# Transposes of an output projection among the parts of its third sum, and a third block pair in the second gate/up product

## The chip, the cores and the metric

The kernel runs on one core of a Trainium2 chip. The core has TensorE (PE in the profile; its weight loads are PEld), VectorE (DVE), ScalarE (ACT), GpSimd (POOL) and SyncE (SP), each with a queue of its own that it works off in the order in which the scheduler put it at build time. The metric is the device time of one execution in microseconds, as a median over runs.

## What is computed

One layer of a decoder trunk for 256 tokens of width 2048, all in float32: half a SwiGLU feed-forward step, a mixing step with two kinds of heads, and a second half step.

```
x = x + 0.5 * swiglu(rmsnorm(x, ffn1_norm), ffn1_w_gate, ffn1_w_up, ffn1_w_down)   # 2048 -> 5632 -> 2048
h = rmsnorm(x, mix_norm)
a_q, a_k, a_v, m_q, m_k, m_v, m_o, m_i, m_f = split(h @ w_in)
y_a = diff_attention(a_q, a_k, a_v, ...)          # 4 heads, causal, normed per head
y_b = rmsnorm(mlstm(m_q, m_k, m_v, m_i, m_f)) * sigmoid(m_o)   # 4 heads
x = x + concat(y_a, y_b) @ w_out                  # the output projection
x = x + 0.5 * swiglu(rmsnorm(x, ffn2_norm), ffn2_w_gate, ffn2_w_up, ffn2_w_down)
out = rmsnorm(x, final_norm)
```

## The kernel before

**Products.** Every weight matrix is worked on in column blocks of 512 (CW). The rows are taken in k tiles of 128, two of them (UK) to a unit; 2048 rows are eight units. The activations stand transposed (k on the partitions), with the 256 tokens in two halves of 128 (hb). A float32 operand is split in a high part, rounded by ScalarE (L131: wh, xs, xt), and a low part, the remainder, by VectorE (L132: wl and the like). A product is three matmuls: high by high, low by high and high by low (`mms`, L180, L181 and L183). A unit done plainly for one column block costs 12 matmuls of 512 columns.

**Pairs in blocks.** `Paired` works two column blocks at once (wa and wb: gate and up, or two neighbouring blocks of a projection). For the first ns units it replaces the eight products of a 2 x 2 block (two k tiles, two token halves, two column blocks) with seven, at the price of sums of activations and of weights. The sums of activations are made by `sum_pair` and `sums` (four small passes of VectorE and another split); the four tiles and their four sums are A1, B1, A2, B2, S3, S1, S2, S4. The sums of weights are made in place in the tiles named raw. The block pair goes through these steps:

- `leading` goes through the block units by twos (`twos`). For each two it loads raw (L422 and L207), multiplies A1 (slot 0), makes the sums of raw on VectorE (L455), and for the two before it multiplies S1 and adds once more (`second_sum`: by a DMA that accumulates, L471, where there are over three block units, and by VectorE, L473, where there are fewer). Between these steps `Chain.run` lets the pair before, whose last part is still open (`stream`), go on unit by unit.
- `sums` multiplies S2 for each two, loads the rows of wa left out so far (the tile late, L487), adds them to raw by accumulating DMAs on POOL (L508), multiplies the late weights bare by A2 (`bare`), then copies and combines the accumulators (`copied`, L479; L512, L521) and multiplies S3.
- `second` does the remaining units of wa plainly and, between them, B2 and S4 of each block unit (`both`).
- `third` finishes wa, hands its two accumulators to `half`, and does the plain units of wb. It is the stream that the next pair's `run` takes along.

**Order.** The scheduler orders each engine's queue by the place of an instruction in the program, and by readiness in its own model of time. `tc.high_priority(offset=AHEAD)` moves instructions ahead by 400 places, `soon()` (used by `vec` and `act`) by 440. `tc.issue_after(newest[0].ins)` puts those TensorE instructions of its block behind the newest matmul that `mms` wrote. Transposes whose results a later step needs are kept as functions in lists: `pending`, taken by `flush(n)`, and `side`, one at a time by `aside(side)`.

**The second gate/up pair.** In the first feed-forward step the first gate block is plain, with the activations loaded and split on the way (`load_xt`, called two units at a time by `units`). The first up block is plain too; its last five units are the stream of the second pair. Five of the eight units of xp1 have activation sums (NP = 5). `sum_xt` makes them one after another: at load time for the units u >= KD // UK - NP_FIRST, queued on ScalarE behind the weight split three before; the others are put on `pending` and are all taken at u == FLUSH of the up stream. The second pair has NP_FIRST block units, later pairs have NP. The raw tiles come from a pool of five, and the first three pairs load them on SP's queue.

**The output projection.** `yT` has eight units: 0 to 3 from the attention heads (transposed by `y_transposes` from `side`), 4 to 7 from the other heads, put on `pending` by `gate_out`. `gate_out(0)` runs as the `half` and `gate_out(1)` as the end of the pair before, whose stream is worked off in the leading steps of the output projection's first pair. That pair is called with `gently=True` and has three block units (NP_OUT), so units 3 to 7 are plain. Each leading step ends with a `flush(1)` behind the newest matmul and with an `aside(side)`; `second` flushes one in each round.

Of the kernel before, what the change touches and what calls it, by code (L numbers as in the profile page):

```python
# [9 lines left out]
F32 = mybir.dt.float32  # L10
F32R = mybir.dt.float32r
BF16 = mybir.dt.bfloat16
AF = mybir.ActivationFunctionType
ALU = mybir.AluOpType
# [18 lines left out]
UK = 2  # L33
# [2 lines left out]
NPS_MIX = (3,4,4,4,3)  # L36
NP_QK = 2
NP_OUT = 3
NP_FIRST = 2
PARTS = (3, 2, 3, 3)  # L40
NP_DOWN = (3, 2, 3, 3)
LK = 4
AHEAD = 400
# [16 lines left out]
def tile_trunk_layer(ctx: ExitStack, tc: tile.TileContext, x, xt, par, bias_if, lamv, fnorm,  # L60
                     wg1, wu1, wd1, wqk0, wqk1, wqk2, win, wout, wg2, wu2, wd2, out):
    nc = tc.nc
# [14 lines left out]
    def nm(s):  # L77
        uid[0] += 1
        return f"{s}_{uid[0]}"
# [16 lines left out]
    def seeded(which):  # L96
        return ps_acc.tile([P, CW], F32, tag=f"acc{which}", name=nm(f"acc{which}"), bufs=1)
# [26 lines left out]
    def split_gain(src, gcol, hi, lo):  # L124

        nc.scalar.activation(hi, src, AF.Copy, scale=prm[:, gcol:gcol + 1])
        nc.vector.scalar_tensor_tensor(lo, src, prm[:, gcol:gcol + 1], hi.bitcast(F32),  # L127
                                       op0=ALU.mult, op1=ALU.subtract)

    def split(src, hi, lo):  # L130
        return (nc.scalar.copy(hi, src),  # L131
                nc.vector.tensor_tensor(out=lo, in0=src, in1=hi.bitcast(F32), op=ALU.subtract))  # L132
# [11 lines left out]
    def ahead_of_splits(i, ins, slack=SLACK):  # L144
        queued[i].append((len(splits) + slack, ins))
# [28 lines left out]
    newest = []  # L174
# [16 lines left out]
    def plain_pair(xp, j):  # L191

        t = slots.tile([P, 2, UK, S], F32R, tag="s", name=nm("xt"))
        xp[j] = tuple(t[:, i, :, :].rearrange("p a (b c) -> p (a b) c", b=NT) for i in range(2))
        return t[:, 0, :, :], t[:, 1, :, :]
# [3 lines left out]
    def flush(n=None):  # L199

        now = pending[:n]
        del pending[:n]
        for f in now:
            f()
# [77 lines left out]
    def chunk_to_xt(c, gbase, xp, ns, now=KD):  # L282


        def run(j):
            tr = ps_tr.tile([P, 2, S], F32, tag="tr", name=nm("tr"))
            for i in range(2):
                for hb in range(NT):
                    nc.tensor.transpose(tr[:, i, hb * P:(hb + 1) * P],
                                        xres[:, hb, (2 * j + i) * P:(2 * j + i + 1) * P], ident)  # L290
            with tc.high_priority(offset=AHEAD):
                if j < ns:
                    sum_pair(xp, j, gained(tr, prm[:, gbase + 2 * j:gbase + 2 * j + 2]), j >= now)
                else:
                    hi, lo = plain_pair(xp, j)
                    for i in range(2):
                        split_gain(tr[:, i, :], gbase + 2 * j + i, hi[:, i, :], lo[:, i, :])

        pending.extend(functools.partial(run, j) for j in (2 * c, 2 * c + 1))
# [4 lines left out]
    def gained(src, gain):  # L304
        g = wk("xg")
        for i in range(2):
            ahead_of_splits(0, act.activation(g[:, i * S:(i + 1) * S], src[:, i, :], AF.Copy, scale=gain[:, i:i + 1]))
        return g.rearrange("p (a b) -> p a b", b=P)

    def sum_tiles(xp, j):  # L310
        xp[j] = tuple(slots.tile([P, 8, P], F32R, tag="s", name=nm("xs")) for _ in range(2))
        return xp[j]

    def sum_pair(xp, j, g, put_off=False):
        hi, lo = sum_tiles(xp, j)
        split(g, hi[:, 0:4, :], lo[:, 0:4, :])
        (side.append if put_off else lambda f: f())(functools.partial(sums, g, hi, lo))

    def sums(g, hi, lo):
        s = wk("xsum").rearrange("p (a b) -> p a b", b=P)  # L320
        tt = nc.vector.tensor_tensor
        tt(out=s[:, 0:2, :], in0=g[:, 0:2, :], in1=g[:, 1:4:2, :], op=ALU.subtract)
        tt(out=s[:, 2, :], in0=s[:, 1, :], in1=g[:, 0, :], op=ALU.subtract)
        tt(out=s[:, 3, :], in0=g[:, 2, :], in1=s[:, 2, :], op=ALU.add)
        split(s, hi[:, 4:8, :], lo[:, 4:8, :])
# [36 lines left out]
    def wk(name):  # L362
        return work.tile([P, CW], F32, tag="w", name=nm(name))
# [11 lines left out]
    def soon(extra=40):  # L375
        return tc.high_priority(offset=AHEAD + extra)
# [14 lines left out]
    vec, act = Early(nc.vector), Early(nc.scalar)  # L391
    side, mid = [], []

    def aside(work):

        if work:
            work.pop(0)()

    class Paired:
# [94 lines left out]
                splits.append(split_weights(raw[:, 0:len(js), :], *t))  # L494
            mms([self.job(self.n11, j, A2, t, i, False, False, True) for i, j in enumerate(js)])

        def sums(self):

            ds = self.copied(self.d, wk("ds"))
            lates = []  # L500
            for js in self.twos:
                lates.append((js, self.late(js)))
                self.part(js, self.x, S2, 0)
                if self.rest[0] // UK not in self.xp:
                    flush(1)
                with tc.high_priority(offset=AHEAD):
                    for i, j in enumerate(js):
                        nc.gpsimd.dma_start(self.raws[j][:, 0, :], lates[-1][1][:, i, :], accum_op=ALU.add)  # L508
                if js[-1] == self.ns - 1:
                    us = self.copied(self.x, wk("us"))  # L510
                    with soon():
                        ahead_of_splits(1, nc.vector.tensor_tensor(out=self.d, in0=self.d, in1=us, op=ALU.subtract))  # L512
                if len(lates) > 1:
                    self.bare(*lates.pop(0))
            for js, raw in lates:
                self.bare(js, raw)
            for js in self.twos:
                self.part(js, self.x, S3, 1)
            self.n21 = self.copied(self.x, seeded(N21), SLACK - 2)
            with soon():  # L520
                ahead_of_splits(1, nc.vector.tensor_tensor(out=self.x, in0=ds, in1=self.x, op=ALU.subtract))  # L521
# [51 lines left out]
    class Chain:  # L573
# [7 lines left out]
        def run(self, p, half, end, last_units=1, gently=False):  # L581

            done = 0
            q = len(p.twos)
            first = p.leading()
            for i in range(q):
                while done < min(self.steps - 1, -(-(i + 1) * self.steps // (q + 1))):
                    next(self.stream)
                    done += 1
                next(first)  # L590
                if gently:
                    with tc.issue_after(newest[0].ins):
                        flush(1)
                else:
                    flush(1)
                aside(side)
            while done < self.steps - 1:
                next(self.stream)
                done += 1
            next(first, None)  # L600
            while done < self.steps:
                next(self.stream)
                done += 1
            self.end()
            p.sums()
            p.second(gently)
            self.put(p.third(half, last_units), len(p.rest) + 1, lambda: end(p.accs()))

# [6 lines left out]
    def ffn(chain, xp, rstd, wg, wu, wd, finish, first=None):  # L615
# [28 lines left out]
        for part, (n, ns) in enumerate(zip(PARTS, NP_DOWN)):  # L644
            hid = {}
            for c in range(n):
# [9 lines left out]
                else:  # L656
                    np_, queue = NP, nc.sync if done + c < ON_POOL else nc.gpsimd
                    if done + c == 1 and first is not None:
                        np_ = NP_FIRST
                        pending.extend([first[1]] * (NP - NP_FIRST))  # L660
                    chain.run(Paired(xp, wg[done + c], wu[done + c], KD, np_, queue=queue), half, end)
# [16 lines left out]
    def load_xt(u):  # L678
        k, i = u * UK, u % 2 * UK
        with tc.high_priority(offset=AHEAD):  # L680
# [14 lines left out]
            for t in range(UK):  # L695
                split_gain(raw[:, t, :], G_FFN1 + k + t, hi[:, t, :], lo[:, t, :])
        if u >= KD // UK - NP_FIRST:
            sum_xt()
# [6 lines left out]
    def sum_xt():  # L705

        raw, j, hi, lo = gs.pop(0)
        with tc.high_priority(offset=AHEAD), tc.issue_after(splits[-FIRST_SUMS][0].ins):
            sums(gained(raw, prm[:, G_FFN1 + j * UK:G_FFN1 + j * UK + UK]), hi, lo)
# [303 lines left out]
    for hb in range(NT):  # L1013
        for h in range(NH):
            i = hb * NH + h
# [49 lines left out]
    yT = {}  # L1065

    def y_transposes(halves, kt, gain):

        g = gain[:, kt % 8:kt % 8 + 2]
        tr = ps_tr.tile([P, 2, S], F32, tag="tr", name=nm("tr"))  # L1070
        for i in range(2):
            for hb in range(NT):
                nc.tensor.transpose(tr[:, i, hb * P:(hb + 1) * P], halves[hb][:, i * P:(i + 1) * P],
                                    ident)
        if kt // 2 < NP_OUT:
            sum_pair(yT, kt // 2, gained(tr, g))
            return
        hi, lo = plain_pair(yT, kt // 2)
        for i in range(2):
            act.activation(hi[:, i, :], tr[:, i, :], AF.Copy, scale=g[:, i:i + 1])  # L1080
            vec.scalar_tensor_tensor(lo[:, i, :], tr[:, i, :], g[:, i:i + 1], hi[:, i, :].bitcast(F32),
                                           op0=ALU.mult, op1=ALU.subtract)

    def weighted(h):
        ps = ps_acc.tile([P, NT, VD], F32, tag="acc", name=nm("av"))
# [43 lines left out]
    for c in (0, 2):  # L1129
        chain.run(Paired(yT, wout[c], wout[c + 1], KD, NP_OUT), functools.partial(finish_out, c),  # L1130
                  functools.partial(finish_out, c + 1),
                  gently=not c)
# [108 lines left out]
```

## Time and profile before

| what | value |
| --- | --- |
| median of three runs | 1772.36 us (1769.11 to 1775.43) |
| the profiled execution | 1771.66 us, of which its span is 1770.0 us |
| granted TensorE clock | 0.998 |
| POOL's busy share | 24% |
| read from HBM | 349.56 MB, 199 GB/s over the span |

The profile shows one execution. A busy share is that of an engine's whole span; a row of the timeline gives the start, the time shown for one or several instructions of a kind, the engine, the line, and in brackets the idle time ahead of it with the instruction that ended it. The time shown for a matmul is modelled and overlaps that of the next, and the same holds in part for VectorE and ScalarE, so the cost of an instruction in a full queue is the distance from its start to the next one's. VectorE and ScalarE share the splitting, and their results go to TensorE through rings of four or five buffers, so a wait on one of them reaches TensorE only if the ring runs empty.

### The profile page before, as it was taken

How to read it: one execution, taken by the hardware profiler on the slowest of the kernel's cores; microseconds unless marked ns; L12 is line 12 of the kernel's file. 1: busy time of each engine (PE TensorE's matmuls, PEld its weight loads, DVE VectorE, ACT ScalarE, POOL GpSimd, SP SyncE). 2: the span in 40 equal slices, each digit the busy share in tenths (PEclk: the TensorE clock that was granted, in tenths of full speed). 3: DMA queues.
4: the chain of work that ended last, by engine and by line, in shares of the span. 5: the costliest groups of instructions: out<-in, count | busy, mean ns of one | idle time of the engine just before them, and what ended most of it. 6: DMA issues, size and time to landing. Idle time of an engine off the chain costs nothing.

```text
span 1770.0 us, 24416 instructions
## 1 busy us (share of the span) xinstructions
PE 1753.1 (99%) x7942; PEld 1439.5 (81%) x7942; DVE 1606.2 (91%) x2168; ACT 1261.5 (71%) x1931; POOL 417.9 (24%) x614
## 2 busy tenths in 40 slices
PE   9999999999999999999999999999999999999998
PEld 6888888888888888987888788878888878888886
DVE  6989999999999999897888899999999999999997
ACT  7676777777667768776776677776677777667765
POOL 0022332322233312111221102122332332233310
PEclk9999999999999999999999999999999999999999
DMA  9788998999799967576766667897988999798984
GB/s 344 257 241 222 249 274 256 265 281 272 209 254 275 274 218 208 188 232 201 219 203 191 187 205 221 236 274 238 247 254 284 234 276 269 237 246 254 267 269 118
DMA packets 153296, 427.08 MB, mean 241 GB/s; under 512 B 17392, under 2 KB 18448, under 8 KB 152912
## 3 DMA queue, kind: packets, MB, share of 16 engines
q0 software_dynamic: 74192, 191.68, 43.0%
q1 hardware_dynamic: 77824, 231.76, 38.5%
q10 hardware_dynamic: 1152, 2.09, 0.3%
q8 instruction: 62, 1.02, 0.2%
q14 instruction: 66, 0.54, 0.1%
HBM read 349.56 MB, written 2.10 MB: 199 GB/s over the span
## 4 chain that ended last, share of the span: by engine, by line
PE 92%; DVE 3%; DMA 2%; issue 2%; ACT 1%; POOL 0%; SPq 0%; POOLq 0%; DVEq 0%; ACTq 0%
PE acc L183 18%; PE acc L180 18%; PE acc L181 18%; PE accn L180 12%; PE accn L181 12%; PE accn L183 12%; DVE wl L132 2%; PE tr L350 1%; DMA raw<-raw 1%; DMA xraw<-in_xt_dram 1%; DMA raw<-in_wg_dram 0%; ACT wh L131 0%; DMA late<-in_wg_dram 0%; PE sc L1034 0%; DMA raw<-in_wu_dram 0%
## 5 line engine op out<-in xcount | busy, mean ns | idle before, releaser
L131 ACT CAST wh<-raw 128x512 fp32r<-128x512 f32 (+2 forms) x865 | 582.7, 707 | 248.9 <-PE acc L181 75.9
L132 DVE TENSOR_TENSOR wl<-raw,wh 128x512 fp32r<-128x512 f32 (+2 forms) x865 | 659.3, 795 | 66.5 <-ACT wh L131 61.4
L132 DVE TENSOR_TENSOR wl<-rawp,wh 128x1024 fp32r<-128x1024 f32 (+3 forms) x316 | 374.0, 1199 | 42.1 <-ACT wh L131 38.0
L131 ACT CAST wh<-rawp 128x1024 fp32r<-128x1024 f32 (+3 forms) x316 | 322.8, 1035 | 93.9 <-PE acc L181 45.5
L180 PE MATMUL acc<-wh,xs 128*128 128x512 f32 (+2 forms) x924 | 357.9, 388 | 0.5 <-ACT us L479 0.5
L181 PE MATMUL acc<-wh,xs 128*128 128x512 f32 (+2 forms) x924 | 357.1, 387 | 0.5 <-DVE xs L132 0.5
L183 PE MATMUL acc<-wl,xs 128*128 128x512 f32 (+2 forms) x924 | 307.5, 388 | 1.1 <-DVE wl L132 0.8
L508 POOL DMA_DIRECT2D raw<-late x172 | 149.1, 1044 | 439.6 <-DVE wl L132 383.7
L180 PE MATMUL acc<-wh,xt 128*128 128x512 f32 (+2 forms) x592 | 228.5, 387 | 0.7 <-ACT wh L131 0.7
L181 PE MATMUL acc<-wh,xt 128*128 128x512 f32 (+2 forms) x592 | 227.6, 385 | 0.0
L180 PE MATMUL accn<-wh,xt 128*128 128x512 f32 (+1 forms) x576 | 227.1, 397 | 0.1
L181 PE MATMUL accn<-wh,xt 128*128 128x512 f32 (+1 forms) x576 | 223.1, 390 | 0.0
L455 DVE TENSOR_TENSOR raw<-raw 128x1024 f32<-128x1024 f32 (+1 forms) x172 | 207.1, 1219 | 0.3
L183 PEld LDWEIGHTS acc<-wl,xs 128*128 128x128 f32 x924 | 172.5, 188 | 39.7 <-DVE wl L132 4.9
L180 PEld LDWEIGHTS acc<-wh,xs 128*128 128x128 f32 x924 | 173.5, 188 | 36.5 <-ACT us L479 1.1
L181 PEld LDWEIGHTS acc<-wh,xs 128*128 128x128 f32 x924 | 173.5, 188 | 35.3 <-DVE xs L132 1.1
L183 PE MATMUL acc<-wl,xt 128*128 128x512 f32 (+2 forms) x592 | 164.6, 385 | 0.0
L183 PE MATMUL accn<-wl,xt 128*128 128x512 f32 (+1 forms) x576 | 161.5, 388 | 0.0
L180 PE MATMUL accn<-wh,xs 128*128 128x512 f32 (+1 forms) x392 | 153.7, 393 | 2.7 <-ACT wh L131 2.1
L181 PE MATMUL accn<-wh,xs 128*128 128x512 f32 (+1 forms) x392 | 151.9, 388 | 0.2 <-DVE xs L127 0.2
L471 POOL DMA_DIRECT2D raw<-raw x86 | 73.6, 872 | 314.5 <-DVE wl L132 239.6
L183 PE MATMUL accn<-wl,xs 128*128 128x512 f32 (+1 forms) x392 | 135.8, 389 | 0.0
(229 smaller groups left out, 2136.6 us busy)
## 6 DMA issues: line engine op xcount, KB each, us to landing
rawp<-in_wd_dram SPq DMA_DIRECT2D x88, 512.0 KB, 5.5
raw<-late POOLq DMA_DIRECT2D x170, 256.0 KB, 5.3
raw<-in_wu_dram POOLq DMA_DIRECT2D x80, 512.0 KB, 7.8
rawp<-in_wu_dram SPq DMA_DIRECT2D x74, 512.0 KB, 5.3
rawp<-in_wg_dram SPq DMA_DIRECT2D x70, 512.0 KB, 5.1
raw<-in_wd_dram POOLq DMA_DIRECT2D x44, 512.0 KB, 7.8
rawp<-in_win_dram SPq DMA_DIRECT2D x44, 512.0 KB, 5.1
raw<-raw POOLq DMA_DIRECT2D x86, 256.0 KB, 4.2
```

The source lines that it names most:

```text
L131: return (nc.scalar.copy(hi, src), nc.vector.tensor_tensor(out=lo, in0=src, in1=hi.bitcast(F32), op=ALU.subtract))
L132: nc.vector.tensor_tensor(out=lo, in0=src, in1=hi.bitcast(F32), op=ALU.subtract))
L180: nc.tensor.matmul(acc, lh, rh, start=first, stop=False, skip_group_check=on)
L181: nc.tensor.matmul(acc, ll, rh, start=False, stop=False, skip_group_check=on)
L183: newest[:] = [nc.tensor.matmul(acc, lh, rl, start=False, stop=last, skip_group_check=on)]
L350: nc.tensor.transpose(tr[:, i, hb * P:(hb + 1) * P], hs[hb][:, k * P:(k + 1) * P], ident)
L455: nc.vector.tensor_tensor(out=raw[:, 0:2, :], in0=raw[:, 0:3:2, :], in1=raw[:, 1:2, :].to_broadcast([P, 2, n]), op=ALU.add)
L471: nc.gpsimd.dma_start(raw[:, 0, :], raw[:, 2, :], accum_op=ALU.add)
L508: nc.gpsimd.dma_start(self.raws[j][:, 0, :], lates[-1][1][:, i, :], accum_op=ALU.add)
```

## The change

Two things are changed. The constant NP_FIRST goes from 2 to 3: the second gate/up pair takes three units in blocks and five plainly. As a consequence one more of the five activation sums is made at load time (at u = 5 as well as 6 and 7), and two, not three, are left on `pending`.

In the output projection's first pair (`gently`), the leading steps no longer flush. The flush of one function now stands in `sums`, behind each part of S2, and behind the newest matmul. The condition that was there before still holds for the other pairs, and their flush in `sums` stands behind the newest matmul now too. In `y_transposes` the splits of the transposed tiles have priority AHEAD: those of the sums had none before, those of the plain units had that of `soon()`.

```
-NP_FIRST = 2
+NP_FIRST = 3
...
-        def sums(self):
+        def sums(self, gently):
...
                 self.part(js, self.x, S2, 0)
-                if self.rest[0] // UK not in self.xp:
-                    flush(1)
+                if gently or self.rest[0] // UK not in self.xp:
+                    with tc.issue_after(newest[0].ins):
+                        flush(1)
...
                 next(first)
-                if gently:
-                    with tc.issue_after(newest[0].ins):
-                        flush(1)
-                else:
-                    flush(1)
+                flush(0 if gently else 1)
                 aside(side)
...
-            p.sums()
+            p.sums(gently)
...
-        if kt // 2 < NP_OUT:
-            sum_pair(yT, kt // 2, gained(tr, g))
-            return
-        hi, lo = plain_pair(yT, kt // 2)
-        for i in range(2):
-            act.activation(hi[:, i, :], tr[:, i, :], AF.Copy, scale=g[:, i:i + 1])
-            vec.scalar_tensor_tensor(lo[:, i, :], tr[:, i, :], g[:, i:i + 1], hi[:, i, :].bitcast(F32),
-                                           op0=ALU.mult, op1=ALU.subtract)
+        with tc.high_priority(offset=AHEAD):
+            if kt // 2 < NP_OUT:
+                sum_pair(yT, kt // 2, gained(tr, g))
+                return
+            hi, lo = plain_pair(yT, kt // 2)
+            for i in range(2):
+                nc.scalar.activation(hi[:, i, :], tr[:, i, :], AF.Copy, scale=g[:, i:i + 1])
+                nc.vector.scalar_tensor_tensor(lo[:, i, :], tr[:, i, :], g[:, i:i + 1], hi[:, i, :].bitcast(F32),
+                                               op0=ALU.mult, op1=ALU.subtract)
```

## The prediction

> **What bounds the kernel now.** I read the page's busy table first, then TensorE's own instructions in order of time to find where its stream has gaps, then who each gap waits for, and last VectorE and ScalarE in those two places.
>
> ```profile
> span 1770.0 us, 24416 instructions
> ...
> PE 1753.1 (99%) x7942; PEld 1439.5 (81%) x7942; DVE 1606.2 (91%) x2168; ACT 1261.5 (71%) x1931; POOL 417.9 (24%) x614
> ...
> PE 92%; DVE 3%; DMA 2%; issue 2%; ACT 1%; POOL 0%; SPq 0%; POOLq 0%; DVEq 0%; ACTq 0%
> ```
>
> TensorE is busy for 99% of the span and makes 92% of the chain that ended last. So there are only two ways to gain: fewer matmuls, or gaps closed in TensorE's stream. VectorE, at 91%, is the engine that can make new gaps. The whole span has 1770.0 - 1753.1 = 16.9 us of idle TensorE. A real gap is a little longer than its idle time, because a matmul is shown as lasting 0.39 us while the next starts far sooner:
>
> ```profile
> 978.98 1.07 PE L183 MATMUL acc<-wl,xt 128*128 128x512 f32 x4
> 979.89 0.39 PE L180 MATMUL acc<-wh,xt 128*128 128x512 f32 x1
> ```
>
> Four matmuls take 979.89 - 978.98 = 0.91 us, so one 512-wide matmul costs **0.227 us** of an undisturbed stream. A gap's loss below is always the distance of two starts less what stands between at that pitch.
>
> The stages of the change, by the windows view (length, then busy time of PE, PEld, DVE, ACT, POOL) and by the TensorE timeline of the output projection:
>
> ```profile
> 14.00:30.00 16.00, 15.85 (x69) 12.64 (x70) 15.86 (x29) 14.61 (x25) 0.00 (x0) 1.00 1.00 397
> 30.00:55.00 25.00, 25.00 (x112) 20.71 (x111) 17.68 (x29) 16.96 (x26) 0.71 (x1) 1.00 0.83 288
> 55.00:70.00 15.00, 14.72 (x68) 11.54 (x67) 13.01 (x17) 12.53 (x19) 1.93 (x2) 1.00 0.76 235
> ...
> 975.00:1000.00 25.00, 21.46 (x98) 16.38 (x97) 22.01 (x40) 15.68 (x30) 2.71 (x4) 1.00 0.42 110
> ...
> 1020.00:1047.00 27.00, 27.00 (x124) 22.25 (x123) 25.74 (x39) 21.82 (x39) 2.67 (x3) 1.00 0.54 148
> ```
>
> ```profile
> 975.03 0.39 PE L180 MATMUL acc<-wh,xt 128*128 128x512 f32 x1
> 976.46 0.30 PE L1073 MATMUL tr<-ident,yb 128*128 128x128 f32 x1 [1.04 <-DVE yb L387]
> ...
> 986.78 0.60 PE L1073 MATMUL tr<-ident,ya 128*128 128x128 f32 x4
> ...
> 987.45 1.09 PE L183 MATMUL acc<-wl,xt 128*128 128x512 f32 x4
> 989.29 0.50 PE L180 MATMUL acc<-wh,xt 128*128 128x512 f32 x1 [0.75 <-ACT wh L131]
> ...
> 994.91 0.61 PE L183 MATMUL accn<-wl,xs 128*128 128x512 f32 x2
> 996.07 0.50 PE L181 MATMUL acc<-wh,xs 128*128 128x512 f32 x1 [0.54 <-DVE xs L132]
> ...
> 996.87 0.40 PE L183 MATMUL acc<-wl,xs 128*128 128x512 f32 x1
> 998.48 0.50 PE L180 MATMUL accn<-wh,xs 128*128 128x512 f32 x1 [1.21 <-ACT wh L131]
> ```
>
> The second gate/up pair (30 to 70 us) loses almost nothing. The start of the output projection has 25.00 - 21.46 = 3.54 us of idle TensorE, a fifth of all there is, in four gaps. Their losses: (a) 976.46 - 975.03 - 0.23 = 1.20; (b) 989.29 - 987.45 - 4 x 0.227 = 0.93; (c) 996.07 - 994.91 - 2 x 0.227 = 0.71; (d) 998.48 - 996.87 - 0.23 = 1.38. Together **4.2 us**. The other pair of the output projection (1020 to 1047 us), also three pairs in blocks, has none.
>
> **Part 1: a third pair in blocks (NP_FIRST 3).** One pair of k tiles done plainly is 8 products, in blocks 7, and each product is three matmuls. So 3 matmuls go: 3 x 0.227 = **-0.68 us** on the path. On the Trainium skill's page "TensorE: Matmul & The Clock Gate", section Back-to-back issue gap, N=512 in a stream of weight loads and matmuls is given as about 131 ns each, and the isolated gap as N / 2.4 + 2.5, about 216 ns; by the first the estimate would be -0.39 us, by the second -0.65. The row above disagrees with the first and is near the second; the measurement decides.
>
> What it costs VectorE and ScalarE, from rows of the same stage:
>
> ```profile
> 41.86 0.42 DVE L322 TENSOR_TENSOR xsum<-xg 128x256 f32<-128x256 f32 x1
> 42.20 0.29 DVE L324 TENSOR_TENSOR xsum<-xg,xsum 128x128 f32<-128x128 f32 x1
> ...
> 44.06 1.29 DVE L132 TENSOR_TENSOR xs<-xsum,xs 128x512 fp32r<-128x512 f32 x2
> 45.27 1.29 DVE L132 TENSOR_TENSOR wl<-raw,wh 128x512 fp32r<-128x512 f32 x2
> 46.47 1.22 DVE L455 TENSOR_TENSOR raw<-raw 128x1024 f32<-128x1024 f32 x1
> 47.60 1.23 DVE L132 TENSOR_TENSOR wl<-rawp,wh 128x1024 fp32r<-128x1024 f32 x1
> ```
>
> ```profile
> 43.57 1.14 ACT L131 CAST wh<-raw 128x512 fp32r<-128x512 f32 x2
> 44.62 1.05 ACT L131 CAST wh<-rawp 128x1024 fp32r<-128x1024 f32 x1
> ```
>
> By distances of starts a 512-wide weight split costs VectorE 0.60 us ((46.47 - 45.27) / 2) and a 1024-wide pass 1.13. ScalarE pays 0.52 ((44.62 - 43.57) / 2) for 512; for 1024 I take 1.05 - 0.10 = 0.95. The plain pair needs two 1024-wide splits; the block pair needs seven splits of 512, one raw sum of 1024 and one of 512 (below four pairs both sums are VectorE's, not DMAs). VectorE: 7 x 0.60 + 1.13 + 0.60 - 2 x 1.13 = **+3.67 us**. ScalarE: 7 x 0.52 - 2 x 0.95 = +1.74 us. On the queues: SP issues the same weights in other pieces and one more load of late; POOL issues one more accumulation raw<-late.
>
> Against that, one of the three activation sums left for the up stream moves into the gate's first stream. It is worth 0.34 + 2 x 0.29 + 0.60 = 1.5 us of VectorE at most (its three small passes and the split), so the stage's net is about **+2.2 us of VectorE**. Its cover is VectorE's idle time, 25.00 - 17.68 = 7.3 us before 55 us and 15.00 - 13.01 = 2.0 us after. Most of the first lies before 39 us and can't be kept, so I count about 3 us of cover: enough, barely. I take 0; the bounds are 0 and the whole 3.67.
>
> The moved sum comes at u = 5 and is queued on ScalarE behind the split of unit 1. That is where both engines wait for loads:
>
> ```profile
> 12.02 1.05 ACT L131 CAST wh<-raw 128x1024 fp32r<-128x1024 f32 x1 [1.75 <-DMA raw<-in_wg_dram]
> ```
>
> ```profile
> 13.11 1.23 DVE L132 TENSOR_TENSOR wl<-raw,wh 128x1024 fp32r<-128x1024 f32 x1 [1.58 <-ACT wh L131]
> ```
>
> In a hole of 1.58 us the 1.5 us cost nothing. If the scheduler places them after 14 us, where VectorE is busy for 15.86 of 16 us, they cost up to 1.5 us. I take 0, because ScalarE is free just there.
>
> Two waits could come. The new accumulation is read by the pair's last split; this run shows what one costs, by ScalarE's timeline and by the view of the tile late (its accumulations between 40 and 80 us):
>
> ```profile
> 64.18 1.05 ACT L131 CAST wh<-raw 128x1024 fp32r<-128x1024 f32 x1 [2.06 <-DMA raw<-late]
> ```
>
> ```profile
> DMA to landing us min/median/max: 6.9/7.0/7.1
> ```
>
> ScalarE waited 2.06 us and TensorE has no gap there, since its plain units go on meanwhile; with three pairs the last accumulation has one more unit of cover. So 0, bounded by 2.06. The page "DMA: Bandwidth & Descriptors" of the Trainium skill, section Anatomy of one DMA, fits such a transfer as 2.0 us plus bytes / 436e3, an estimate of 2.6 us for 256 KB, by which that wait would be gone; the row has 6.9 to 7.1. The other wait is a buffer: the third pair's loads find one raw buffer fewer free, and SP stands behind that load. SP is idle there anyway:
>
> ```profile
> 54.07 0.71 SPq L207 DMA_DIRECT2D raw<-in_wu_dram  x1
> 65.54 0.80 SPq L218 DMA_DIRECT2D rawp<-in_wg_dram  x2
> ```
>
> It issues nothing for 10.8 us, so I take 0 here too.
>
> **Part 2: transposes of the output projection.** Two groups of four yb transposes leave the leading steps for a place behind the parts of the third sum. TensorE still does them (0.60 us for four as shown above, some 0.4 us of the stream by starts: 987.45 less 986.78 less one matmul), so their own time neither goes nor comes. What goes with them is in ScalarE's queue:
>
> ```profile
> 986.46 0.48 ACT L387 ACTIVATE xt<-tr,prm 128x256 fp32r<-128x256 f32 x1 [3.93 <-PE tr L1073]
> ...
> 987.46 0.48 ACT L387 ACTIVATE xt<-tr,gatt 128x256 fp32r<-128x256 f32 x1
> 987.83 0.48 ACT L387 ACTIVATE xt<-tr,prm 128x256 fp32r<-128x256 f32 x1
> 988.18 1.05 ACT L131 CAST wh<-rawp 128x1024 fp32r<-128x1024 f32 x1
> ...
> 996.84 0.59 ACT L479 COPY ds<-acc 128x512 f32<-128x512 f32 x1 [3.03 <-PE acc L183]
> 997.32 0.59 ACT L479 COPY us<-acc 128x512 f32<-128x512 f32 x1
> 997.79 0.63 ACT L131 CAST wh<-late 128x512 fp32r<-128x512 f32 x1
> ```
>
> ScalarE stands 3.93 us for a transpose, and behind it waits the split whose product TensorE lacks at gap (b). By gap: (a) waits for the yb that is now transposed later; the ya of that place was ready before, so it closes: -1.20. (b) The two activations of yb leave (2 x 0.37 by starts), but the ya transposes stay and ScalarE may stand for them instead; between 0 and -0.93 I take -0.5. (c) waits for a split of activation sums that had no priority and now has: -0.7. (d) is ScalarE's copies of the sum and then the late weights' split; four transposes (0.4 us) now fill part of it, while their splits queue on the same engine: between +1.5 (four activations of 0.37 ahead of the late split) and -1.38 I take -0.4. Sum **-2.8 us**, bounds -4.2 and about +1.5 (nothing closes and (d) grows).
>
> The flushes in sums of other pairs now stand behind the newest matmul too. TensorE's stream there goes on with the bare products and the S3 parts, so I count nothing; without that cover it would be one wait like (d), 1.4 us a place.
>
> **Sum:** -0.68 - 2.8 = -3.5 us. The profiled execution took 1771.66 us (span 1770.0 and 1.66 around it), which gives 1768.2. The median of the three runs, 1772.36, stands 0.7 above it, so the forecast against that is **1768.9 us**. One measurement of this kernel can tell about 0.3%, 5.3 us, from no change: faster is below 1767.0, slower above 1777.7.
>
> **The rivals.**
> *The wait only moves.* The splits of the moved transposes stand in ScalarE's queue ahead of the late split, so what (a) and (b) give is lost at (d). For it: the 3.93 us shows that this queue waits in order. Against: ScalarE idles 3.03 us just before those copies, room for four activations. Only the matmuls stay gained: 1772.36 - 0.7 = 1771.7 us. The page "PSUM — Partial Sum Buffer" of the Trainium skill, section Engine vs sequencer instructions, has ScalarE's queue strictly first in, first out; by that rule this rival can happen, and the 3.93 us agrees.
> *All closes.* Four gaps go (-4.2), the matmuls (-0.68), and the small loss at the second gate/up pair's sums, whose row of idle is 15.00 - 14.72 = 0.28 us: -5.2, or 1767.2 us; with the runs' own scatter about half of this case reads as faster than the bound.
> *Slower: VectorE becomes the bound at 40 to 75 us.* If its idle time there can't be moved, all of 3.67 us goes on TensorE's end less the 0.68, +3.0, and the moved sum adds 1.5 at the start: 1776.9 us with nothing gained in part 2. It decides from the point at which the stage's +2.2 us exceeds the some 3 us of usable idle. Against it: the other three-pair stage (1020 to 1047 us) keeps TensorE at 27.00 of 27.00 us with VectorE at 25.74.
>
> **How the numbers follow.** Forecast 0.55, the wait moves 0.20, all closes 0.17, slower 0.08. The three before runs lie 3.3 below and 3.1 above their median, so about 2 us of scatter goes on each case. The range 1765.0 to 1775.0 takes in the first three with that scatter and leaves out the slower rival's far end. Faster by over 0.3%: half of all closes plus the forecast's lower tail, 0.17. Slower by over 0.3%: half of its rival, 0.04. Within: 0.79.
>
> **What would show it.** Right: three matmuls fewer before 100 us, no idle at TensorE's yb transposes, ScalarE's 3.93 us gone, and idle TensorE between 975 and 1000 us at about 1.3 instead of 3.54 us. Wrong: new rows of TensorE waiting for VectorE's wl between 45 and 75 us or after 14 us; a gap over 1.4 us after the second S2 part; ScalarE standing for the ya transposes as long as before. What would upset the whole forecast is a different order of instructions in stages that the change doesn't name.

## The result, and the profile after

The changed kernel takes 1768.64 us (median of 16 runs, 1765.92 to 1771.09); the kernel before, run beside it, 1771.23 us (16 runs). The ratio is 0.9982, with a 95% interval from 0.9974 to 0.9990. By the ratio that is 3.2 us faster (1.8 to 4.6); the two medians differ by 2.6. It is inside the forecast range, and close to the forecast gain of 3.5. The ratios in this document leave out two runs that took far longer, one of the kernel before (2953.72 us) and one of the kernel with two pairs and three early sums (6287.37 us; its median without that run is 1768.26 us). The total is not the proof of its terms, though: one part gained more than I had said, and the other lost what it was to save.

The page of the changed kernel, first the busy table:

```profile
span 1767.5 us, 24438 instructions
...
PE 1751.7 (99%) x7939; PEld 1439.4 (81%) x7939; DVE 1609.0 (91%) x2174; ACT 1263.8 (72%) x1935; POOL 419.3 (24%) x615
```

Three matmuls fewer (7939 for 7942), six more VectorE instructions with 2.8 us more busy time (I had worked out 3.67 us of cost, by distances of starts), and one more DMA issued by POOL. TensorE's idle time hardly moved in all: 1767.5 - 1751.7 = 15.8 us, against 16.9. So the gain isn't one clean subtraction, and the windows view (length, then busy time of PE, PEld, DVE, ACT, POOL) shows two stages that go opposite ways:

```profile
14.00:30.00 16.00, 14.84 (x64) 11.66 (x63) 15.45 (x27) 13.54 (x23) 0.00 (x0) 1.00 1.02 414
...
55.00:70.00 15.00, 14.98 (x69) 11.81 (x68) 14.56 (x21) 13.25 (x21) 2.75 (x3) 1.00 0.85 229
...
975.00:1000.00 25.00, 24.47 (x116) 19.95 (x115) 24.41 (x43) 18.73 (x35) 4.28 (x4) 1.00 0.44 112
```

In the output projection 3.54 us of idle TensorE are now 0.53. From 14 to 30 us 0.15 us of idle are now 1.16, although the DMAs are as busy there as before. The second pair's stage (55 to 70 us) shows no new idle time: 0.02 us, for 0.28. TensorE's timeline of the changed kernel has the places, and behind it VectorE's the split that the third row waits for:

```profile
19.30 0.73 PE L180 MATMUL accn<-wh,xs 128*128 128x512 f32 x2 [0.38 <-ACT xs L126]
...
20.81 0.50 PE L181 MATMUL accn<-wh,xs 128*128 128x512 f32 x1 [0.78 <-DVE xs L127]
...
985.61 0.50 PE L181 MATMUL acc<-wh,xs 128*128 128x512 f32 x1 [0.53 <-DVE xs L132]
...
995.53 0.60 PE L1070 MATMUL tr<-ident,yb 128*128 128x128 f32 x4
...
996.65 0.60 PE L1070 MATMUL tr<-ident,yb 128*128 128x128 f32 x4
```

```profile
984.87 0.69 DVE L132 TENSOR_TENSOR xs<-xg,xs 128x512 fp32r<-128x512 f32 x1
...
988.22 0.69 DVE L132 TENSOR_TENSOR xs<-xsum,xs 128x512 fp32r<-128x512 f32 x1
```

The yb transposes stand in the third sum without a wait. The output projection's four gaps are gone, and one wait of 0.53 us is new: not for the split of sums (xs<-xsum), which gap (c) was, but for that of the third unit's own four tiles (xs<-xg). The two waits at the start are new as well. My sign for trouble there, TensorE waiting for VectorE's wl, named the wrong tile: it waits for the split of activations.

To compare stages over all kernels I use **lost time**: for every matmul the distance to the next start, less the median distance for its width (0.227 us at 512 columns), summed over a stage. The start is everything up to 60 matmuls before the first transposes of gate times up (tr<-ident,sg), the second pair the 310 matmuls from there on, the output projection the stretch from 30 matmuls before the first ya transposes to 130 behind the last. All in us, worked out from the starts in each trace:

```
kernel                              start  second pair  output proj.  all the rest
before                               2.67      0.91         5.19         13.40
before, second profile               2.60      0.91         6.56         15.53
after                                3.18      0.83         1.43         14.74
after, second profile                3.99      0.84         1.43         14.01
third pair alone                     4.07      0.83         5.20         15.00
output projection's edits alone      1.67      0.91         1.42         10.84
priority alone                       2.12      0.90         2.01         12.89
moved flushes alone                  1.86      0.99         4.44         11.41
three pairs, two early sums          1.91      1.67         1.44         11.97
two pairs, three early sums          3.60      0.13         1.42         13.09
priority of the sums' splits alone   2.55      0.91         2.06         12.94
three pairs, third sum put later     2.73      1.64         1.45         11.84
other pairs' flushes alone           2.16      0.91         5.22         11.88
```

I take the last column for chance for the most part: the same program differs by 2.1 us between two profiles of before. The output projection's figure repeats within 0.03 us wherever the program there is the same, but for one row that is explained at the end; its level hangs on the pitch taken for the attention's products and the transposes in that stretch, the differences between kernels do not. The second pair's figure repeats within 0.01 us in the two profiles of each program that has two. The start's does not: it differs by 0.8 us between the two profiles of the changed kernel. So the two later stages can be told apart by one profile each, the start only by the place of its loss, and totals only by the timed runs. The profile after has one more thing that I had not looked for: two gaps of 1.2 us each in a later gate/up pair, near 360 us, which the profile before lacks. Some of the experiments ask whether the change makes them.

### The profile page after: what moved, and what is told of

Same layout as the page of the kernel before. It is cut to its first block, busy times and chain, and to the rows that moved or that the text cites. A ratio compares the mean times of both kernels' runs of the same rounds, so it can differ in the third digit from the quotient of the medians.

```text
span 1767.5 us, 24438 instructions
## 1 busy us (share of the span) xinstructions
PE 1751.7 (99%) x7939; PEld 1439.4 (81%) x7939; DVE 1609.0 (91%) x2174; ACT 1263.8 (72%) x1935; POOL 419.3 (24%) x615
## 5 line engine op out<-in xcount | busy, mean ns | idle before, releaser
L455 DVE TENSOR_TENSOR raw<-raw 128x1024 f32<-128x1024 f32 x173 | 208.0, 1216 | 0.3
```

The costliest lines, as they stand in the source:

```text
L455: nc.vector.tensor_tensor(out=raw[:, 0:2, :], in0=raw[:, 0:3:2, :], in1=raw[:, 1:2, :].to_broadcast([P, 2, n]), op=ALU.add)
```

## The experiments

**The third pair alone.** The constant, nothing else.

```
-NP_FIRST = 2
+NP_FIRST = 3
```

> Only the third pair in blocks (NP_FIRST 3), the output projection as before. Theory 1 (the two parts add up): three matmuls fewer, 0.68 us, against some 0.5 us more lost at the start, where the sum of u = 5 falls into VectorE's full stretch; so within 1 us of before, ratio 0.9993 to 1.0003, and the four gaps of the output projection stay, with about 3.5 us of idle TensorE in the 25 us behind its yb transposes' place. Rival (the earlier order shifts later stages): those gaps change too, and the time falls by 2 us or more.

Measured: 1772.66 us against 1771.17 for before, ratio 1.0007 (0.9998 to 1.0015). The four gaps of the output projection are all there (lost 5.20 us), so the parts don't act on each other; that much of theory 1 holds. But the ratio is above the band that it gave (though its interval reaches into the band): the third pair gains nothing, and by the medians it costs 1.5 us.

**The output projection's edits alone.** The changed kernel with the constant back at 2.

```
-NP_FIRST = 3
+NP_FIRST = 2
```

> Only the output projection's edits and the flush in sums, NP_FIRST 2. Theory 1: nearly the whole gain is here, 2 to 3.8 us, ratio about 0.998 to 0.9989; idle TensorE in that stretch falls from 3.54 us to about 0.5, and the start is as before. Rival (both parts are needed, or the gain is chance): less than 1 us.

Measured: 1766.83 us, ratio 0.9975 (0.9963 to 0.9986). All of the gain is here, and by its median this kernel is faster than the changed one (1768.64), though the intervals of the two ratios overlap. Idle TensorE between 975 and 1000 us is 0.52 us, and the start loses 1.67 us.

**Priority alone, and the moved flushes alone.** The output projection's edits taken apart. The first keeps the flushes where they were and puts only the splits of `y_transposes` ahead:

```
+        with tc.high_priority(offset=AHEAD):
+            if kt // 2 < NP_OUT:
+                sum_pair(yT, kt // 2, gained(tr, g))
...
```

> Only the priority AHEAD in y_transposes; the flushes stay in the leading steps. Theory 1 (the place does most): gap (c), TensorE waiting for the split of activation sums, closes or shrinks, 0.7 us; ScalarE still stands some 4 us for the yb transposes and gaps (a), (b), (d) stay, so 0 to 1 us faster than before. Rival (the priority does it all): 2.5 us or more, and the stand of ScalarE is gone.

The second has the changed flushes in `sums` and `Chain.run`, with `y_transposes` as before.

> Only the moved flush, with the splits' priorities as before and NP_FIRST 2. Theory 1: gap (a) closes and ScalarE's 3.9 us are gone, (c) stays, (d) is partly filled; 1.5 to 2.5 us faster than before. Rival (priority does it all): within 1 us of before, with the wait at the third sum as long as what was removed.

Measured: priority alone 1766.88 us, ratio 0.9971 (0.9960 to 0.9982); the move alone 1770.11 us, ratio 0.9994 (0.9985 to 1.0003). My theory falls here, and the rival stands: the priority does nearly all of it. In lost time of the output projection, 5.19 goes to 2.01 by priority (-3.18), to 4.44 by the move (-0.75), and to 1.43 by both (-3.76, nearly their sum). The priority kernel's gap and ScalarE's stand, from its TensorE and ScalarE timelines:

```profile
978.42 0.30 PE L1073 MATMUL tr<-ident,yb 128*128 128x128 f32 x1 [0.69 <-DVE yb L387]
...
984.35 0.60 PE L1073 MATMUL tr<-ident,yb 128*128 128x128 f32 x4
```

```profile
979.31 0.48 ACT L1081 ACTIVATE xt<-tr,prm 128x256 fp32r<-128x256 f32 x1 [3.57 <-PE tr L1073]
...
984.80 1.05 ACT L131 CAST wh<-rawp 128x1024 fp32r<-128x1024 f32 x1
985.75 0.48 ACT L1081 ACTIVATE xt<-tr,prm 128x256 fp32r<-128x256 f32 x1
...
992.17 0.58 ACT L479 COPY ds<-acc 128x512 f32<-128x512 f32 x1
992.64 0.63 ACT L131 CAST wh<-late 128x512 fp32r<-128x512 f32 x1
993.16 0.63 ACT L131 CAST wh<-raw 128x512 fp32r<-128x512 f32 x1
993.68 0.60 ACT L479 COPY us<-acc 128x512 f32<-128x512 f32 x1
```

Gap (a) is the only one left. ScalarE still stands 3.57 us for a yb transpose, but not at the place of the 3.93 us: this stand is for the first group of transposes (978.42), where the kernel before stands 1.01 us (its ScalarE timeline, at 977.46). At the second group (984.35), where the 3.93 us were, there is none. The weight split that stood behind it in the kernel before, at 988.18, now comes at 984.80, ahead of the activation of yb at 985.75, and (b) is gone. So the rival's sign, the stand gone, holds where it mattered. And the late split now runs at 992.64, before the copy us at 993.68; in the kernel before it came behind us, so that gap (d) was the way from the last S2 product over two copies and a split. The moved kernel, on the other side, by its TensorE timeline:

```profile
983.62 0.50 PE L181 MATMUL acc<-wh,xs 128*128 128x512 f32 x1 [0.86 <-DVE xs L132]
...
994.08 0.50 PE L181 MATMUL acc<-wh,xs 128*128 128x512 f32 x1 [0.20 <-DVE xs L132]
...
995.13 0.60 PE L1070 MATMUL tr<-ident,yb 128*128 128x128 f32 x4
...
996.87 0.50 PE L180 MATMUL accn<-wh,xs 128*128 128x512 f32 x1 [1.14 <-ACT wh L131]
```

Here (a) is gone and of (b) 0.18 us are left, but TensorE waits twice for splits of activation sums, the first time (983.62) where the kernel before had no gap, and (d) is as long as ever, with the transposes at 995.13 ahead of it. Its ScalarE timeline says why these fill nothing:

```profile
995.34 0.59 ACT L479 COPY us<-acc 128x512 f32<-128x512 f32 x1
995.82 0.49 ACT L387 ACTIVATE xt<-tr,prm 128x256 fp32r<-128x256 f32 x1
996.18 0.63 ACT L131 CAST wh<-late 128x512 fp32r<-128x512 f32 x1
```

An activation of yb stands between the copy us and the late split and puts the split off by 0.36 us, which is what four transposes take in TensorE's stream (995.53 to 995.88 in the changed kernel).

**Which splits.** In `y_transposes`, priority for the sums' splits only; the plain units' as before.

```
         if kt // 2 < NP_OUT:
-            sum_pair(yT, kt // 2, gained(tr, g))
+            with tc.high_priority(offset=AHEAD):
+                sum_pair(yT, kt // 2, gained(tr, g))
             return
```

> The kernel before with priority for the splits of the three activation sums in y_transposes alone; the splits of the plain units and all flushes as before. Theory 1 (those splits, which had no priority, held the queue): the whole effect of the priority, 3 to 5 us faster than before, idle TensorE in the 25 us behind the first yb transposes' place under 1 us. Rival (it is the lowered priority of the plain units' splits, from 440 to 400 places): within 1 us of before.

Measured: 1767.48 us, ratio 0.9982 (0.9973 to 0.9991), lost time of the output projection 2.06 us, like 2.01 with all of them. TensorE's timeline has gap (a) again (0.70 us idle) and no other wait. So it is the splits of the three units with sums, which had no priority at all. VectorE's timeline has the last of them, in the kernel before and in the kernel with priority for all:

```profile
995.33 0.69 DVE L132 TENSOR_TENSOR xs<-xsum,xs 128x512 fp32r<-128x512 f32 x1
```

```profile
985.23 0.68 DVE L132 TENSOR_TENSOR xs<-xsum,xs 128x512 fp32r<-128x512 f32 x1
```

Ten microseconds earlier; the third unit's S2 product needs it. How the lower priority of these splits held up the others, (b) and (d) among them, is read off the changed order of the queues; it was not taken further apart.

**The place of the sums at the start.** Two kernels part the third pair from its early sum. First the changed kernel with only two sums at load time:

```
-        if u >= KD // UK - NP_FIRST:
+        if u >= KD // UK - 2:
             sum_xt()
...
-                        pending.extend([first[1]] * (NP - NP_FIRST))
+                        pending.extend([first[1]] * (NP - 2))
```

> The changed kernel with three block pairs, but only two activation sums at load time as before the change (the third waits for the up stream). Theory 1 (the loss of the pair is the early sum, whose splits meet VectorE's full stretch at the start): the start's loss falls from 3.2 to about 2 us, the matmuls stay saved, so 1 to 1.5 us faster than the changed kernel, about 1767. Rival (the third block pair itself costs, through later loads): no faster than the changed kernel, with the two gaps near 360 us again.

The other way round: two pairs in blocks, with the output projection's edits, but three early sums (NP_FIRST 2 and the two conditions above with 3).

> The output projection's edits with two block pairs, but three activation sums at load time. Theory 1: it pays the start's loss without the saved matmuls, so 1 to 1.5 us slower than the kernel with the output projection's edits alone (1766.8), and no gap near 360 us. Rival (the early sum is harmless): like that kernel, within 0.5 us.

Measured: three pairs with two early sums 1766.13 us, ratio 0.9973 (0.9963 to 0.9982); two pairs with three early sums 1768.62 us, ratio 0.9985 (0.9976 to 0.9994). Theory 1 holds in both for the start, and the medians move its way; the intervals of the timed ratios overlap, with that of the changed kernel (0.9974 to 0.9990) in the first case and with that of the output projection's edits alone (0.9963 to 0.9986) in the second. The start loses 3.2 to 4.1 us in all three programs with three early sums (the changed kernel, the third pair alone, and this one), and 1.7 to 2.7 in all others. All four profiles of the former have 1.5 us of loss at the same place, by matmuls that start between 18.5 and 20.2 us; none of the others has any there. ScalarE's order there, first of the changed kernel, then of the output projection's edits alone:

```profile
10.01 0.91 ACT L387 ACTIVATE xg<-xraw,prm 128x256 f32<-128x256 f32 x2
...
16.47 0.91 ACT L387 ACTIVATE xg<-xraw,prm 128x256 f32<-128x256 f32 x2
17.28 0.61 ACT L131 CAST xs<-xsum 128x512 fp32r<-128x512 f32 x1
17.79 1.05 ACT L131 CAST wh<-rawp 128x1024 fp32r<-128x1024 f32 x1
18.75 0.90 ACT L126 ACTIVATE xs<-xraw,prm 128x256 fp32r<-128x256 f32 x2
```

```profile
16.58 0.91 ACT L387 ACTIVATE xg<-xraw,prm 128x256 f32<-128x256 f32 x2
17.39 0.89 ACT L126 ACTIVATE xs<-xraw,prm 128x256 fp32r<-128x256 f32 x2
```

With three sums the split of a sum and a weight split come between, and the activations of unit 4 (xs, L126) are split 1.36 us later, at 18.75 for 17.39. TensorE waits for just these (its rows at 19.30 and 20.81 above).

But the second pair's figure moves the other way. With three pairs it is 1.67 us after a start in time and 0.83 after a late one; with two pairs 0.91 and 0.13. So the third pair has a price of its own, 0.7 to 0.8 us at either start, and a late start takes some 0.8 us off the stage with two pairs as with three. The kernel before against the changed one (0.91 and 0.83) shows neither, because the two cancel.

**A better place for the third sum.** The changed kernel with two sums at load time, and the third behind the gate's last weight split, where both engines run ahead of TensorE:

```
-                    half(linear(xp, wg[0], KD, ahead=first[0], in_pieces=True,
-                                banks=[functools.partial(seeded, b) for b in (N11, N21)]))
+                    ag = linear(xp, wg[0], KD, ahead=first[0], in_pieces=True,
+                                banks=[functools.partial(seeded, b) for b in (N11, N21)])
+                    first[1](1)
+                    half(ag)
...
-    def sum_xt():
+    def sum_xt(behind=FIRST_SUMS):
...
-        with tc.high_priority(offset=AHEAD), tc.issue_after(splits[-FIRST_SUMS][0].ins):
+        with tc.high_priority(offset=AHEAD), tc.issue_after(splits[-behind][0].ins):
```

> The changed kernel with three block pairs, two activation sums at load time and the third queued behind the gate's last weight split, where VectorE and ScalarE are ahead of TensorE. Theory 1 (only the place of the sum costs): the start loses about 2 us as with two sums, the second pair at most 0.9, and the matmuls stay saved; about 1765.5, 3 us faster than the changed kernel. Rival (three sums before the up stream always cost their 1.5 us): about 1768, as the changed kernel.

Measured: 1767.33 us, ratio 0.9981 (0.9973 to 0.9990), less than hoped, and by time not to be told from the changed kernel (0.9982). The trace decides between the two. The start's loss from 18.5 to 20.5 us is gone (its 2.73 us lie at the first loads), but the second pair loses 1.64 us again, in one gap:

```profile
54.68 0.50 PE L180 MATMUL acc<-wh,xt 128*128 128x512 f32 x1 [0.71 <-ACT wh L131]
```

```profile
47.33 0.62 ACT L131 CAST wh<-raw 128x512 fp32r<-128x512 f32 x1 [0.86 <-DVE raw L455]
52.01 0.62 ACT L131 CAST wh<-raw 128x512 fp32r<-128x512 f32 x1 [4.06 <-DVE raw L455]
53.10 0.57 ACT L479 COPY accn<-acc 128x512 f32<-128x512 f32 x1 [0.47 <-PE acc L183]
53.58 1.05 ACT L131 CAST wh<-rawp 128x1024 fp32r<-128x1024 f32 x1
```

```profile
30.00:45.00 15.00, 15.00 (x68) 12.41 (x67) 9.07 (x17) 12.91 (x19) 0.71 (x1) 1.00 0.96 377
45.00:52.00 7.00, 7.00 (x33) 5.79 (x32) 7.00 (x9) 2.09 (x4) 0.00 (x0) 1.00 0.31 93
```

ScalarE stands 4.06 us for VectorE's weight sums (L455), and a plain unit's split comes behind them. By the windows view VectorE is busy for all of 7.00 us from 45 to 52 us, and idle for 5.93 of the 15 us before that. Where the third activation sum was made no longer matters: it is the pair's own work on VectorE. The changed kernel has the same stand of 4.06 us, and no gap; its TensorE comes through the start later. The same holds for the kernel with the third pair alone.

**The other pairs' flushes alone.** The kernel before with the flush of the other pairs in `sums` behind the newest matmul.

```
                 if self.rest[0] // UK not in self.xp:
-                    flush(1)
+                    with tc.issue_after(newest[0].ins):
+                        flush(1)
```

> The kernel before with one edit: the flush in sums of the other pairs stands behind the newest matmul. Theory 1 (it costs and gains nothing, because the bare products and S3 follow): within 1 us of before, the output projection's loss unchanged at 5.2 us. Rival (it gives part of the gain, or takes 1.4 us a place): 1.5 us or more to either side.

Measured: 1771.58 us against 1771.11, ratio 1.0001 (0.9991 to 1.0010), as theory 1 has it.

**The same programs again.** One more profile of the changed kernel and one of the kernel before.

> The changed kernel unchanged, for a second profile. If the gaps near 360 us belong to the program, they are there again (about 1.1 us each); if they are chance, that stretch loses under 1 us. The start's loss should again be 3 to 4 us, the output projection's about 1.4.

> The kernel before, unchanged, for a second profile: the losses that belong to the program (5.2 us in the output projection, about 0.9 in the second pair) come again; those of the start, of the stretch near 360 us and of the one near 1160 us, which hang on when loads land, may differ by a microsecond or two.

The changed kernel took 1769.41 us and lost 3.99 us at the start and 1.43 in the output projection. The gap near 360 us, which in its first profile came twice, came once (1.27 us); the kernel before, which had none in its first profile, has it in the second, and so has the kernel with the sums' splits ahead, which has two pairs (1.13 us):

```profile
365.34 0.50 PE L183 MATMUL acc<-wl,xs 128*128 128x512 f32 x1 [0.99 <-DVE wl L132]
```

So it belongs to neither program: what first looked like a stall that the third pair makes 300 us later is chance. What sets it off was not settled; in the five profiles with the gap the loads of 256 KB that POOL issues for this pair land in 9.0 to 10.7 us (medians), in the eight without it in 6.7 to 8.2.

## Why the prediction was right, and where it wasn't

The number was right: -3.5 us forecast, -3.2 measured. By its steps:

- **Three matmuls, -0.68 us.** Right: three instructions fewer.
- **The third pair's splits and sums at 0.** The cover wasn't enough. They cost 0.7 to 0.8 us of the stage (1.67 against 0.91 us lost with the start in time, 0.83 against 0.13 with a late one), as much as the matmuls save: three pairs with two early sums and two pairs, both with the output projection's edits, can't be told apart (ratios 0.9973 and 0.9975). I had counted on some 3 us of idle VectorE; in the kernel with the third sum put later it lies before 45 us, and from there to 52 us there is none. The mechanism that I gave to the slower rival, VectorE as the bound from 40 to 75 us, is there with about a fifth of the price of 3.67.
- **The moved activation sum at 0, at most 1.5.** This step failed, at its upper end. The first passes did fall into the hole that I had pointed to (xg at 10.01 us on ScalarE), but the sum's split came later, in the full stretch, and pushed unit 4's activations 1.36 us back. I had looked for room for 1.5 us of work and not at where a chain of seven instructions over two engines ends (two activations for xg, three passes of VectorE, and the two halves of the split). It costs 1.5 us, the whole of my bound.
- **The new wait for an accumulation and the raw buffer at 0.** No gap of TensorE in the second pair has either as its releaser.
- **Gap (a), -1.20.** Right, and by the move, as said: priority alone leaves 0.85 us there.
- **Gap (b), -0.5, by ScalarE's stand.** It closes wholly (0.93 us), in the kernel with priority alone and, but for 0.18 us, in the moved kernel. The way that I read, a split that stands in ScalarE's queue behind the stand of 3.93 us, agrees with both: in neither does the split stand behind it any more (in the moved kernel a stand of 2.62 us for VectorE, at 985.20, is ahead of the split instead, and 0.18 us of the gap are left). What I missed is that the move isn't needed for it: priority alone puts the split ahead of the activation of yb.
- **Gap (c), -0.7, by priority.** Right, in the kernel with priority alone. With both edits it closes too, but a new wait of the same length stands at 985.61 (0.53 us idle, for 0.54), for the split of the third unit's own tiles. I had not counted it; in the changed kernel's sum it cancels (c).
- **Gap (d), -0.4, partly filled by transposes.** Wrong. Transposes alone fill nothing (1.14 us idle stay in the moved kernel), since an activation of yb puts the late split off by as much. With the priority (d) closes wholly; in its rows the late split comes ahead of the copy us.
- **Sum of the output projection, -2.8.** Measured -3.8 in lost time, between my value and the bound of -4.2: all four gaps close, and the new wait takes 0.7 back. Without the third pair the kernel is 4.4 us faster (2.5 to 6.5), and the whole change 3.2.
- **The other pairs' flushes at 0.** Right, measured alone.
- **The rival that the wait only moves.** It is most of what the move alone does: (a) and (b) are worth 2.1 us, and 0.75 are gained (ratio 0.9994). Its mechanism, an activation of yb ahead of the late split, is there with 0.36 us; the larger loss is a new wait of 1.03 us for a split of sums, at 983.62, which the rival didn't name. The priority, which I had counted for 0.7 us, is what keeps the rival from winning.

So the total was met because two errors cancel: some 1 us too little for the output projection, and some 2 us too much for the pair. Within the output projection I had given the move most of a gain that the priority alone makes. That the number came out is luck; the gaps and their sum were read rightly, their causes only in part. The fastest programs of the study are the output projection's edits without the early sum: priority alone (0.9971), three pairs with two early sums (0.9973), the edits with two pairs (0.9975). Each is faster than before clear of its interval, and by its median 1.8 to 2.5 us faster than the changed kernel; their intervals overlap with that of the changed kernel and with one another.

## What to carry to other kernels

Before moving work to another place, look which instructions on the way to the waiting product have the lowest priority in their queue: here three groups of splits without any priority cost 3 us, and moving the transposes around them 0.75. A hole in an engine's timeline takes a chain of instructions only if its last one ends there; count the chain's end, not its busy time. When an edit gains at one stage and loses at another, time each part alone, and compare a stage only among kernels that reach it equally late: here a late start took 0.8 us off the next stage and so covered a price of the same size.

## What the runs showed that was not expected

In the second profile of the kernel before, TensorE's granted clock fell to half in the output projection, by the timeline and the windows view (the eighth value, after POOL's, is the granted clock):

```profile
1002.78 0.63 PE L180 MATMUL acc<-wh,xs 128*128 128x512 f32 x1
1003.21 0.63 PE L181 MATMUL acc<-wh,xs 128*128 128x512 f32 x1
```

```profile
1002.00:1005.50 3.50, 3.41 (x9) 2.64 (x10) 3.50 (x6) 3.48 (x6) 0.00 (x0) 0.57 0.75 257
```

Seven matmuls start 0.43 us apart instead of 0.227, which costs 1.4 us: this is what makes the 6.56 in the table out of 5.16, the figure of the first profile but for 0.03. The clock's records put the half speed at a stretch of 3.41 us. In the 3.41 us before it lie most of gap (c) and all of gap (d), 0.73 and 1.39 us lost. The Trainium skill's page "TensorE: Matmul & The Clock Gate", section What's actually happening, names a window of 3413 ns, which agrees with the length, and gives as its condition an idle window; here TensorE had worked for over a third of it. Among the four profiles of programs that keep all four gaps it came once, and never in the nine others. So several gaps close together may cost more than their own length; that these gaps caused the half clock is not shown, by one case and without a trial.
